# Branch outputs loaded and split ahead of the last gates' sigmoids, and both weightings of the dilated groups beside the first projection

## The chip, the cores and the metric

The kernel runs on one core of one Trainium2 chip, as one launch. The metric is the device time in microseconds (us) of one execution. Engines are called PE (TensorE), ACT (ScalarE), DVE (VectorE), POOL (GpSimd) and SP (SyncE); SP, POOL and ACT also issue DMAs from their queues.

## The reference, cut to what matters

One layer of an encoder, sequence 1024, width 1024, all in float32. From the normalized input `n` come three branches: A, dilated window attention in three head groups (dilation 1, 4, 16), whose group outputs are weighted by a softmax over their log-sum-exps; B, retention; C, cross-attention into 256 memory tokens. Each branch output is projected to 1024 columns, multiplied by a sigmoid gate and summed:

```python
alpha = jax.nn.softmax(jnp.stack(lses, axis=0), axis=0)
y = jnp.stack(outs, axis=0) * alpha[..., None].astype(q.dtype)
...
gates = jax.nn.sigmoid(n @ w_gate + b_gate).reshape(B, S, N_BRANCHES, D_MODEL)
merged = (gates[:, :, 0] * (y_a @ w_proj_attn)
          + gates[:, :, 1] * (y_r @ w_proj_ret)
          + gates[:, :, 2] * (y_m @ w_proj_mem))
h = h + merged @ w_out
```

A gated MLP with a short convolution and a final norm follow.

## The kernel before

All large products are made of three matmuls (`mm3`, L177 to L180): each float32 operand is split into a high and a low part, `hilo` (L182): ACT writes the high part (L183), DVE the rest (L184). Weights come by `WStream`: SP loads one of three `wraw` buffers (L222), `hilo` splits it into one of three `wh`/`wl` pairs, always for a column ahead. So each operand of PE passes SP, then ACT, then DVE.

The stage before the change is the gates: 12 pairs of gate columns, seven steps each (`gate_steps`, L1002 to L1065), 84 steps of 12 matmuls, merged evenly by `merge` with the 92 steps of the dilated attention (`attn_dil`). Of the last pair, the last step's sum is the function `late` (DVE at L1059, then two sigmoids on ACT at L1011, and stores to `sg_d` by POOL), called after the merged steps (L1176).

Then come the projections, one branch after the other, in `order`: b0 is retention (6 parts of 128 rows), b1 memory (4 parts), b2 the dilated attention (6 parts). `proj_steps` (L1187) has a step `begin`, in which `y_part` (L1069) loads each part of the branch output from DRAM into a `yraw` tile by SP and splits it into `yh` and `yl`, and eight steps `one(c)`, a column block each: 2 x 3 matmuls for each part into two PSUM banks (`accg`, six banks, so three columns), then DVE multiplies with the gate, loaded as `sg` by POOL (L1200), and adds to `mg`. The `yraw` tiles share the three buffers of the weights:

```python
r = W.rp.tile([P, S], F32, name="yraw", tag="wraw", bufs=3)
nc.sync.dma_start(r, y_src[bi][k * P:(k + 1) * P, :])
```

The 12 tiles of `yh`/`yl` are a pool `y_p`, opened after the gates. `sg`, the three U tiles of a weighting, and gate results are in the pool `ab` of eight buffers.

The weighting of the dilated groups is `combine(s)` (L885), for s = 0 and 1: `lse` (POOL loads three U tiles; ACT takes a logarithm, L896), `bcast(g)` for each group (DVE spreads the values into `lw`, L905, PE transposes them, L910, ACT copies them into L), and `comb(h)` for each half: maxima (L923, L924), differences (L926), exponentials on ACT (L927), products with U (L935), sums, two reciprocals (L931), products (L936), and stores into `ya_d` (L937), by POOL for s = 0 and by ACT's queue for s = 1. Its 12 steps are merged with the 18 steps of b0 and b1:

```python
run(merge(proj_steps(b0, k0) + proj_steps(b1, k1), combine(0, stats, cb_p) + combine(1, stats, cb_p)))
run(proj_steps(b2, k2))
```

A scheduler sets the final order of instructions on each engine; each engine then takes its queue in that order.

Of the kernel before, what the change touches and what calls it, by code (L numbers as in the profile page):

```python
# [11 lines left out]
F32 = mybir.dt.float32  # L12
# [5 lines left out]
P = 128  # L18
D = 1024
S = 1024  # L20
# [45 lines left out]
def merge(a, b):  # L66
    out, i, j = [], 0, 0
    while i < len(a) or j < len(b):
        if j >= len(b) or (i < len(a) and i * len(b) <= j * len(a)):
            out.append(a[i])  # L70
            i += 1
        else:
            out.append(b[j])
            j += 1
    return out


def run(steps):
    for s in steps:
        s()  # L80
# [65 lines left out]
def encoder_block(ctx: ExitStack, tc: tile.TileContext, x, mem, vec, w_mix, w_gate, w_pa, w_pr, w_pm,  # L146
                  w_out, w_mlp, g_final, t_rope, t_mask, t_ret, t_zeta, out):
    nc = tc.nc
# [3 lines left out]
    def pool(name, **kw):  # L152
        kw.setdefault("bufs", 1)
        return tc.tile_pool(name=name, reuse_waits="tile", **kw)
# [260 lines left out]
    pairs = PAIRS  # L415
# [469 lines left out]
    def combine(s, stats, ap_):  # L885
        loc = {}

        def lse():
            loc["st"] = [stats[3 * s + g] for g in range(3)]
            loc["U"] = [ab("U") for g in range(3)]  # L890
            for g in range(3):
                nc.gpsimd.dma_start(loc["U"][g], u_d[(3 * s + g) * P:(3 * s + g + 1) * P, :])
            loc["lse"] = ap_.tile([P, 3, 2, 8], F32, name="lse", tag="lse")
            for g in range(3):
                nc.vector.tensor_copy(loc["lse"][:, g], loc["st"][g][1])
            nc.scalar.activation(loc["lse"], loc["lse"], AF.Ln)  # L896
            for g in range(3):
                nc.vector.tensor_sub(loc["lse"][:, g], loc["lse"][:, g], loc["st"][g][0])
            loc["L"] = []

        def bcast(g):
            L = ap_.tile([P, S], F32, name="L", tag="L", bufs=3)
            for b in range(2):
                W2 = ap_.tile([P, 4, 2, 64], F32, name="lw", tag="sm", bufs=3)
                nc.vector.tensor_copy(W2, loc["lse"][:, g, :, 4 * b:4 * b + 4].rearrange("p h t -> p t h")  # L905
                                      [:, :, :, None].to_broadcast([P, 4, 2, 64]))
                ps = pst()
                for a in range(4):
                    t = 4 * b + a
                    nc.tensor.transpose(ps[:, a * P:(a + 1) * P],  # L910
                                        W2[:, a].rearrange("p a b -> p (a b)"), ident)
                if DIL[g] == 1:
                    nc.scalar.copy(L[:, b * HALF:(b + 1) * HALF], ps)
                else:
                    unperm(L, ps, DIL[g], b)
            loc["L"].append(L)

        def comb(h):
            c = slice(h * HALF, (h + 1) * HALF)
            L = [t[:, c] for t in loc["L"]]  # L920
            m = ap_.tile([P, HALF], F32, name="cm", tag="sm", bufs=3)
            z = ap_.tile([P, HALF], F32, name="cz", tag="sm", bufs=3)
            nc.vector.tensor_tensor(m, L[0], L[1], op=ALU.max)  # L923
            nc.vector.tensor_tensor(m, m, L[2], op=ALU.max)  # L924
            for g in range(3):
                nc.vector.tensor_sub(L[g], L[g], m)  # L926
                nc.scalar.activation(L[g], L[g], AF.Exp)  # L927
            nc.vector.tensor_add(z, L[0], L[1])
            nc.vector.tensor_add(z, z, L[2])
            for a in range(2):  # L930
                nc.vector.reciprocal(z[:, a * 256:(a + 1) * 256], z[:, a * 256:(a + 1) * 256])  # L931
            for g in range(3):
                u = loc["U"][g][:, c]
                k = 2 * g + s
                nc.vector.tensor_mul(u, u, L[g])  # L935
                nc.vector.tensor_mul(u, u, z)  # L936
                (nc.gpsimd, nc.scalar)[s].dma_start(ya_d[k * P:(k + 1) * P, c], u)  # L937

        return [lse] + [lambda g=g: bcast(g) for g in range(3)] + [lambda: comb(0), lambda: comb(1)]


    def attn_mem(h, qm, cp):
# [123 lines left out]

    y_src = {0: ya_d, 1: yr_d, 2: ym_d}

    def y_part(bi, k):  # L1069

        r = W.rp.tile([P, S], F32, name="yraw", tag="wraw", bufs=3)
        nc.sync.dma_start(r, y_src[bi][k * P:(k + 1) * P, :])
        a, b = (y_p.tile([P, S], F32R, name=t, tag="y", bufs=12) for t in ("yh", "yl"))
        hilo(a, b, r)
        return a, b
# [38 lines left out]
    T_s = ExitStack()  # L1114
# [56 lines left out]
    for k in range(KP):  # L1171
        hilo(*T1[k], t1[k])
    gates = sum((gate_steps(p, box, lambda: psW.tile([P, HALF], F32, name="w", tag="w", bufs=4))
                 for p in range(NG)), [])
    run(merge(gates, sum((attn_dil(i, ap_, stats) for i in range(len(pairs))), [])))
    box.pop("late")()  # L1176
    gs.close()
    T_s.close()


    pg = ExitStack()
    psG = pg.enter_context(pool("psG", space=PS))
    psb.update(pool=psG, bufs={"t": 2})
    cb_p = pg.enter_context(pool("cb_p", side="right"))
    y_p = pg.enter_context(pool("y_p"))
    mg = [n_p.tile([P, S], F32, name=f"mg{k}", tag="n", bufs=16) for k in range(KT - 1)] + [ab("mg")]
    mgh, mgl = [], []  # L1187

    def proj_steps(bi, kt):
        loc = {}  # L1190

        def begin():
            loc["y"] = zip(*[y_part(bi, k) for k in range(kt)])
            loc["y"] = list(loc["y"])

        def one(c):
            wh, wl = W.get()
            yh, yl = loc["y"]
            sg = ab("sg")
            nc.gpsimd.dma_start(sg, sg_d[(bi * KT + c) * P:(bi * KT + c + 1) * P, :])  # L1200
            ps = [psG.tile([P, HALF], F32, name="accg", tag="accg", bufs=6) for h in range(2)]
            for k in range(kt):
                for h in range(2):
                    cs = slice(h * HALF, (h + 1) * HALF)
                    mm3(ps[h], wh[:, k], wl[:, k], yh[k][:, cs], yl[k][:, cs], k == 0, k == kt - 1)
            if bi == order[2][0]:
                for r in (mgh, mgl):
                    r.append(n_p.tile([P, S], F32R, name=f"mg{c}", tag="n", bufs=16))
            for h in range(2):
                cs = slice(h * HALF, (h + 1) * HALF)  # L1210
                m = mg[c][:, cs]
                if bi == order[0][0]:
                    nc.vector.tensor_mul(m, ps[h], sg[:, cs])
                else:
                    nc.vector.tensor_mul(sg[:, cs], ps[h], sg[:, cs])
                    nc.vector.tensor_add(m, m, sg[:, cs])
                if bi == order[2][0]:
                    hilo(mgh[c][:, cs], mgl[c][:, cs], m)

        return [begin] + [lambda c=c: one(c) for c in range(KT)]  # L1220

    (b0, _, k0), (b1, _, k1), (b2, _, k2) = order
    run(merge(proj_steps(b0, k0) + proj_steps(b1, k1), combine(0, stats, cb_p) + combine(1, stats, cb_p)))
    run(proj_steps(b2, k2))
    pg.close()
    mk_s.close()

# [468 lines left out]
```

## Time and profile before

| | us |
|---|---|
| median of 3 runs | 1911.7 (1910.52 to 1913.72) |
| the profiled execution: time | 1913.29 |
| the profiled execution: span | 1911.5 |
| PE busy | 1849.1 (97%) |
| DVE busy | 1258.5 (66%) |
| ACT busy | 913.0 (48%) |
| POOL busy | 120.7 (6%) |

The span runs from the first to the last instruction of the one profiled execution. Busy time is the sum of an engine's instructions; a wait shows as idle time before an instruction, with the engine or DMA that ended it. `PEclk` is the granted clock of PE as a share of 2.4 GHz (0.50 is 1.2 GHz). In a timeline, consecutive instructions of one kind stand as one row with their count, and durations overlap by about 0.1 us, since an engine starts the next instruction before the last one's end.

### The profile page before, as it was taken

How to read it: one execution, taken by the hardware profiler on the slowest of the kernel's cores; microseconds unless marked ns; L12 is line 12 of the kernel's file. 1: busy time of each engine (PE TensorE's matmuls, PEld its weight loads, DVE VectorE, ACT ScalarE, POOL GpSimd, SP SyncE). 2: the span in 40 equal slices, each digit the busy share in tenths (PEclk: the TensorE clock that was granted, in tenths of full speed). 3: DMA queues.
4: the chain of work that ended last, by engine and by line, in shares of the span. 5: the costliest groups of instructions: out<-in, count | busy, mean ns of one | idle time of the engine just before them, and what ended most of it. 6: DMA issues, size and time to landing. Idle time of an engine off the chain costs nothing.

```text
span 1911.5 us, 24342 instructions
## 1 busy us (share of the span) xinstructions
PE 1849.1 (97%) x9314; PEld 1534.8 (80%) x9314; DVE 1258.5 (66%) x2192; ACT 913.0 (48%) x1498; POOL 120.7 (6%) x222
## 2 busy tenths in 40 slices
PE   7999999999999999999899699989999999999997
PEld 6889988888887777777687589967888888888886
DVE  7554463657455555555467864575888887899976
ACT  7354342435446556665533233552545454445444
POOL 1000010110000000000101000000000000020001
PEclk9999999999999999999999899989999999999999
DMA  6211111122331333223636525321223222287553
GB/s 245 94 54 45 45 54 47 67 78 89 110 110 67 111 127 115 100 78 110 214 123 214 200 87 186 119 82 54 90 77 100 79 87 89 77 341 264 171 165 116
DMA packets 65988, 223.69 MB, mean 117 GB/s; under 512 B 7760, under 2 KB 7888, under 8 KB 65744
## 3 DMA queue, kind: packets, MB, share of 16 engines
q1 hardware_dynamic: 41760, 138.77, 21.5%
q0 software_dynamic: 22096, 79.70, 11.0%
q10 hardware_dynamic: 2016, 3.67, 0.5%
q8 instruction: 73, 1.20, 0.3%
q14 instruction: 43, 0.35, 0.1%
HBM read 168.64 MB, written 53.48 MB: 116 GB/s over the span
## 4 chain that ended last, share of the span: by engine, by line
PE 91%; DVE 4%; DMA 2%; ACT 2%; issue 1%; POOL 0%; SPq 0%; POOLq 0%; ACTq 0%; DVEq 0%
PE ps L180 11%; PE ps L179 11%; PE ps L178 11%; PE acc L180 8%; PE acc L178 8%; PE acc L179 8%; PE w L178 5%; PE w L179 4%; PE w L180 4%; PE accg L178 2%; PE accg L179 2%; PE accg L180 2%; PE pss L810 2%; PE psu L854 2%; PE pso L179 2%; PE pso L180 2%
## 5 line engine op out<-in xcount | busy, mean ns | idle before, releaser
L183 ACT CAST wh<-wraw 128x1024 fp32r<-128x1024 f32 (+2 forms) x263 | 253.1, 967 | 326.6 <-PE acc L179 80.8
L184 DVE TENSOR_TENSOR wl<-wraw,wh 128x1024 fp32r<-128x1024 f32 (+2 forms) x263 | 293.8, 1118 | 150.0 <-ACT wh L183 145.2
L178 PE MATMUL acc<-nTh,wh 128*128 128x512 f32 x544 | 214.5, 394 | 0.0
L180 PE MATMUL acc<-nTh,wl 128*128 128x512 f32 x544 | 212.7, 391 | 0.0
L179 PE MATMUL acc<-nTl,wh 128*128 128x512 f32 x544 | 212.4, 390 | 0.0
L178 PE MATMUL ps<-wh,th 128*128 128x512 f32 x308 | 119.8, 389 | 0.0
L179 PE MATMUL ps<-wl,th 128*128 128x512 f32 x308 | 119.8, 389 | 0.0
L180 PE MATMUL ps<-wh,th 128*128 128x512 f32 x308 | 119.8, 389 | 0.0
L180 PEld LDWEIGHTS acc<-nTh,wl 128*128 128x128 f32 x544 | 102.2, 188 | 20.4
L178 PEld LDWEIGHTS acc<-nTh,wh 128*128 128x128 f32 x544 | 102.2, 188 | 20.2
L179 PEld LDWEIGHTS acc<-nTl,wh 128*128 128x128 f32 x544 | 102.3, 188 | 19.8
L179 PE MATMUL accg<-yl,wh 128*128 128x512 f32 x256 | 103.4, 405 | 11.2 <-DVE yl L184 11.0
L178 PE MATMUL accg<-yh,wh 128*128 128x512 f32 x256 | 98.8, 404 | 8.6 <-ACT yh L183 8.3
L539 ACT COPY sw<-acc 32x512 f32<-32x512 f32 x144 | 83.4, 579 | 49.1 <-PE acc L180 29.4
L180 PE MATMUL accg<-yh,wl 128*128 128x512 f32 x256 | 102.0, 400 | 0.5 <-DVE wl L184 0.5
L178 PE MATMUL w<-nTh,wh 128*128 128x512 f32 x192 | 79.2, 412 | 0.0
L179 PE MATMUL w<-nTl,wh 128*128 128x512 f32 x192 | 75.1, 391 | 0.0
L180 PE MATMUL w<-nTh,wl 128*128 128x512 f32 x192 | 75.0, 391 | 0.0
L178 PE MATMUL pso<-wh,mg 128*128 128x256 f32 x256 | 73.2, 286 | 0.0
L180 PE MATMUL pso<-wh,mg 128*128 128x256 f32 x256 | 72.5, 283 | 0.0
L179 PE MATMUL pso<-wl,mg 128*128 128x256 f32 x256 | 72.5, 283 | 0.0
L183 ACT CAST th<-g 128x512 fp32r<-128x512 f32 x66 | 40.9, 622 | 64.8 <-PE ps L180 45.4
(387 smaller groups left out, 4561.0 us busy)
## 6 DMA issues: line engine op xcount, KB each, us to landing
wraw<-in_w_mlp_dram SPq DMA_DIRECT2D x90, 512.0 KB, 4.0
wraw<-in_w_mix_dram SPq DMA_DIRECT2D x48, 512.0 KB, 3.5
wraw<-in_w_gate_dram SPq DMA_DIRECT2D x24, 512.0 KB, 3.5
sg<-sg_d POOLq DMA_DIRECT2D x24, 512.0 KB, 5.1
g_d<-cv POOLq DMA_DIRECT2D x22, 512.0 KB, 2.9
g<-g_d POOLq DMA_DIRECT2D x22, 512.0 KB, 14.3
wraw<-in_w_out_dram SPq DMA_DIRECT2D x16, 512.0 KB, 4.0
sg_d<-ub POOLq DMA_DIRECT2D x12, 512.0 KB, 2.9
```

The lines of the kernel that those rows point to most:

```text
L178: nc.tensor.matmul(o, lh, rh, start=first, stop=False, **kw)
L179: nc.tensor.matmul(o, lh, rl, start=False, stop=False, **kw)
L180: nc.tensor.matmul(o, ll, rh, start=False, stop=last, **kw)
L183: nc.scalar.copy(hi, src)
L184: nc.vector.tensor_sub(lo, src, hi.bitcast(F32))
L539: nc.scalar.copy(sw[q * 32:(q + 1) * 32], ps[o * 32:(o + 1) * 32])
L810: nc.tensor.matmul(ps[:, a * w:(a + 1) * w], st["q"][r, q0:q0 + P], st["k"][r, k0:k0 + w], start=True, stop=True)
L854: nc.tensor.matmul(u[64 * i:64 * i + 64, c], loc["V"][:, vslot[k0 + k * P], 64 * i:64 * i + 64], pt[:, k, a], start=k == 0, stop=k == nk - 1)
```

## The change

`combine`'s step `bcast` is cut in two, `spread` (DVE's part) and `bcast` (PE and ACT), so that a weighting has nine steps. The `yraw` tiles move from the weights' buffers to the pool `ab`. The last four gate steps are run after the merged list, which now merges 80 gate steps with the 92 of the attention; three parts of b0 are loaded ahead of those four steps, the pool `y_p` opens after them (in the space of `T_p`, the gates' operands), the rest of b0 is loaded and all of it split, and only then `late` is called. Both weightings, 18 steps, are merged with the nine steps of b0. Two parts of b1 are loaded before b1's steps, four of b2 before its last two.

```diff
-        def bcast(g):
-            L = ap_.tile([P, S], F32, name="L", tag="L", bufs=3)
+        def spread(g):
+            loc["w"] = []
             for b in range(2):
                 W2 = ap_.tile([P, 4, 2, 64], F32, name="lw", tag="sm", bufs=3)
                 nc.vector.tensor_copy(W2, loc["lse"][:, g, :, 4 * b:4 * b + 4].rearrange("p h t -> p t h")
                                       [:, :, :, None].to_broadcast([P, 4, 2, 64]))
+                loc["w"].append(W2)
+
+        def bcast(g):
+            L = ap_.tile([P, S], F32, name="L", tag="L", bufs=3)
+            for b, W2 in enumerate(loc.pop("w")):
                 ps = pst()
...
-        return [lse] + [lambda g=g: bcast(g) for g in range(3)] + [lambda: comb(0), lambda: comb(1)]
+        steps = [lambda g=g, f=f: f(g) for g in range(3) for f in (spread, bcast)]
+        return [lse] + steps + [lambda: comb(0), lambda: comb(1)]
...
-    def y_part(bi, k):
-
-        r = W.rp.tile([P, S], F32, name="yraw", tag="wraw", bufs=3)
+    def y_raw(bi, k):
+        r = ab("yraw")
         nc.sync.dma_start(r, y_src[bi][k * P:(k + 1) * P, :])
+        return r
+
+    def y_part(r):
+
         a, b = (y_p.tile([P, S], F32R, name=t, tag="y", bufs=12) for t in ("yh", "yl"))
         hilo(a, b, r)
         return a, b
...
-    run(merge(gates, sum((attn_dil(i, ap_, stats) for i in range(len(pairs))), [])))
+    b0, b1, b2 = (b for b, _, _ in order)
+    y_r = {}
+
+    def y_load(bi, ks):
+        for k in ks:
+            y_r[bi, k] = y_raw(bi, k)
+
+    run(merge(gates[:-4], sum((attn_dil(i, ap_, stats) for i in range(len(pairs))), [])))
+    y_load(b0, range(3))
+    run(gates[-4:])
+    T_s.close()
+    pg = ExitStack()
+    y_p = pg.enter_context(pool("y_p"))
+    y_hl = {}
+
+    def y_split(bi, kt):
+        y_load(bi, [k for k in range(kt) if (bi, k) not in y_r])
+        y_hl[bi] = list(zip(*[y_part(y_r.pop((bi, k))) for k in range(kt)]))
+
+    y_split(b0, order[0][2])
     box.pop("late")()
     gs.close()
-    T_s.close()
...
         def begin():
-            loc["y"] = zip(*[y_part(bi, k) for k in range(kt)])
-            loc["y"] = list(loc["y"])
+            if bi not in y_hl:
+                y_split(bi, kt)
...
-    (b0, _, k0), (b1, _, k1), (b2, _, k2) = order
-    run(merge(proj_steps(b0, k0) + proj_steps(b1, k1), combine(0, stats, cb_p) + combine(1, stats, cb_p)))
-    run(proj_steps(b2, k2))
+    s0, s1, s2 = (proj_steps(bi, kt) for bi, _, kt in order)
+    run(merge(s0, combine(0, stats, cb_p) + combine(1, stats, cb_p)))
+    y_load(b1, range(2))
+    run(s1[:-2])
+    y_load(b2, range(4))
+    run(s1[-2:] + s2)
```

What a scheduler makes of it is seen in the built order of each engine. Where a row ends in a count, that many follow each other; line numbers behind the change are those of the changed file.

**ACT at the end of the gates, before.** `ub` and `ua` are the last gate pair, `lse` belongs to the first weighting, `wh` are weights of b0.

```order
L1046 COPY ub<-w 128x512
L839 COPY pt_s<-pst 128x256
L183 CAST wh<-wraw 128x768
L883 COPY U<-psu 128x8x64
L1011 ACT_TABLE_LOAD
L1011 ACTIVATE ub<-ub,vec 128x1024
L1011 ACTIVATE ua<-ua,vec 128x1024
L896 ACT_TABLE_LOAD
L896 ACTIVATE lse<-lse 128x48
L183 CAST yh<-yraw 128x1024
L183 CAST wh<-wraw 128x768
```

The same place with the change:

```order
L896 ACT_TABLE_LOAD
L896 ACTIVATE lse<-lse 128x48
L1047 COPY ua<-w 128x512
L1051 COPY ub<-w 128x512
L183 CAST wh<-wraw 128x768
L183 CAST yh<-yraw 128x1024
L1016 ACT_TABLE_LOAD
L1016 ACTIVATE ub<-ub,vec 128x1024
L183 CAST yh<-yraw 128x1024
L1016 ACTIVATE ua<-ua,vec 128x1024
L183 CAST yh<-yraw 128x1024
L183 CAST wh<-wraw 128x768
```

The logarithm has moved ahead of the last copies; one cast of a part of b0 stands ahead of the first sigmoid, one between the two, the other four behind.

**DVE at the split of b1's parts, before** (`yl` are the low halves of the parts, `U`, `cz`, `L`, `cm` the weighting, `mg` and `sg` the products of a column). The end of the first weighting stands here:

```order
L931 RECIPROCAL cz<-cz 128x256 x2
L935 TENSOR_TENSOR U<-U,L 128x512
L1213 TENSOR_TENSOR mg_7825<-accg,sg 128x512 x2
L936 TENSOR_TENSOR U<-U,cz 128x512 x3
L184 TENSOR_TENSOR wl<-wraw,wh 128x512
L184 TENSOR_TENSOR yl<-yraw,yh 128x1024
L184 TENSOR_TENSOR wl<-wraw,wh 128x512
L905 COPY lw<-lse 128x512 x3
L1213 TENSOR_TENSOR mg<-accg,sg 128x512
L184 TENSOR_TENSOR yl<-yraw,yh 128x1024
L1213 TENSOR_TENSOR mg<-accg,sg 128x512
L184 TENSOR_TENSOR yl<-yraw,yh 128x1024 x2
```

The same place with the change, from the first half's last products of the second weighting on:

```order
L940 TENSOR_TENSOR U<-U,cz 128x512 x3
L928 TENSOR_TENSOR cm<-cm,L 128x512
L184 TENSOR_TENSOR yl<-yraw,yh 128x1024
L930 TENSOR_TENSOR L<-L,cm 128x512 x3
...
L935 RECIPROCAL cz<-cz 128x256 x2
L184 TENSOR_TENSOR yl<-yraw,yh 128x1024
L940 TENSOR_TENSOR U<-U,cz 128x512 x3
L184 TENSOR_TENSOR yl<-yraw,yh 128x1024
L184 TENSOR_TENSOR wl<-wraw,wh 128x512
L184 TENSOR_TENSOR yl<-yraw,yh 128x1024
```

Here the second weighting stands, whose second half has come between b1's first and second part, with its last products between the second and third. The first half stands ahead of all of them.

## Rows read from the trace of the kernel before

**Rows 1.** The page's first line, the span of the profiled execution.

```profile
span 1911.5 us, 24342 instructions
```

**Rows 2.** Busy times by stage: gates' end, b0, b1, b2; then PEclk, DMA share, GB/s.

```profile
core 0: us, PE busy (x) PEld busy (x) DVE busy (x) ACT busy (x) POOL busy (x), PEclk, DMA share, GB/s
860.00:936.20 76.20, 76.20 (x378) 58.58 (x376) 39.25 (x107) 46.22 (x86) 6.39 (x12) 1.00 0.39 140
936.20:1017.30 81.10, 73.31 (x318) 59.74 (x318) 51.90 (x82) 26.79 (x33) 10.21 (x19) 0.96 0.45 151
1017.30:1069.30 52.00, 49.16 (x211) 38.64 (x210) 40.07 (x60) 15.44 (x20) 4.38 (x9) 0.93 0.62 223
1069.30:1152.40 83.10, 69.23 (x289) 54.52 (x290) 54.10 (x75) 23.54 (x32) 2.64 (x5) 0.94 0.38 136
```

**Rows 3.** What PE waited for from 936 to 1153: total us, times, longest.

```profile
PE accg L179 <- DVE yl L184: 11.0, 3, 10.0
PE accg L178 <- ACT yh L183: 8.3, 7, 3.4
PE pst L910 <- DVE lw L905: 4.2, 1, 4.2
```

**Rows 4.** The projections' matmuls alone in a steady stretch of b2.

```profile
1100.00:1150.00 50.00, 50.00 (x222) 41.42 (x221) 8.14 (x12) 1.00 0.27 90
```

**Rows 5.** Timeline of PE: start, us, instruction, count [idle before].

```profile
973.27 1.03 PE L910 MATMUL pst<-ident,lw 128*128 128x128 f32 x8
...
1081.64 0.80 PE L179 MATMUL accg<-yl,wh 128*128 128x512 f32 x1 [9.99 <-DVE yl L184]
1082.24 0.63 PE L180 MATMUL accg<-yh,wl 128*128 128x512 f32 x1
1082.66 0.63 PE L179 MATMUL accg<-yl,wh 128*128 128x512 f32 x1
```

**Rows 6.** Timeline of DVE, end of b0's split and the weighting before b2.

```profile
961.89 1.23 DVE L184 TENSOR_TENSOR yl<-yraw,yh 128x1024 fp32r<-128x1024 f32 x1 [1.87 <-ACT yh L183]
...
1069.33 1.89 DVE L926 TENSOR_TENSOR L<-L,cm 128x512 f32<-128x512 f32 x3
...
1077.97 1.89 DVE L936 TENSOR_TENSOR U<-U,cz 128x512 f32<-128x512 f32 x3
...
1080.37 1.22 DVE L184 TENSOR_TENSOR yl<-yraw,yh 128x1024 fp32r<-128x1024 f32 x1
```

**Rows 7.** Timeline of SP's queue, the loads of b2's parts.

```profile
1064.38 26.23 SPq L1072 DMA_DIRECT2D yraw<-ya_d  x6
```

**Rows 8.** Timeline of ACT, end of the gates, and one strided copy pair.

```profile
932.44 0.83 ACT L183 CAST wh<-wraw 128x768 fp32r<-128x768 f32 x1 [2.66 <-PE w L179]
...
934.34 1.28 ACT L1011 ACT_TABLE_LOAD   x1
935.63 1.15 ACT L1011 ACTIVATE ub<-ub,vec 128x1024 f32<-128x1024 f32 x1
...
938.12 1.28 ACT L896 ACT_TABLE_LOAD   x1
939.41 0.24 ACT L896 ACTIVATE lse<-lse 128x48 f32<-128x48 f32 x1
939.79 1.05 ACT L183 CAST yh<-yraw 128x1024 fp32r<-128x1024 f32 x1
...
1039.91 2.04 ACT L883 COPY L<-pst 128x512 f32<-128x512 f32 x2
```

**Rows 9.** The page's DMA issues: KB each, median us from issue to landing.

```profile
sg<-sg_d POOLq DMA_DIRECT2D x24, 512.0 KB, 5.1
```

**Rows 10.** Short stretches; the column before DMA share is PEclk.

```profile
940.00:944.00 4.00, 3.44 (x10) 2.49 (x11) 3.38 (x7) 2.15 (x3) 1.07 (x2) 0.65 0.76 267
...
1082.00:1084.00 2.00, 2.00 (x6) 1.52 (x6) 1.06 (x2) 0.00 (x0) 1.52 (x3) 0.50 0.90 285
1088.00:1092.00 4.00, 3.02 (x12) 1.68 (x11) 1.62 (x2) 2.05 (x2) 0.00 (x0) 1.00 1.03 415
```

More of the change, by code (lines that the diff above doesn't have):

```diff
@@ L906, in bcast @@
                                       [:, :, :, None].to_broadcast([P, 4, 2, 64]))
+                loc["w"].append(W2)
+        def bcast(g):
+            L = ap_.tile([P, S], F32, name="L", tag="L", bufs=3)
+            for b, W2 in enumerate(loc.pop("w")):
                 ps = pst()
                 for a in range(4):
-                    t = 4 * b + a
                     nc.tensor.transpose(ps[:, a * P:(a + 1) * P],
@@ L1174, in encoder_block @@
                  for p in range(NG)), [])
-    run(merge(gates, sum((attn_dil(i, ap_, stats) for i in range(len(pairs))), [])))
+    b0, b1, b2 = (b for b, _, _ in order)
[14 more added lines that the diff above has]
+    y_split(b0, order[0][2])
     box.pop("late")()
     gs.close()
-    T_s.close()
-    pg = ExitStack()
     psG = pg.enter_context(pool("psG", space=PS))
@@ L1184, in encoder_block @@
     cb_p = pg.enter_context(pool("cb_p", side="right"))
-    y_p = pg.enter_context(pool("y_p"))
     mg = [n_p.tile([P, S], F32, name=f"mg{k}", tag="n", bufs=16) for k in range(KT - 1)] + [ab("mg")]
@@ L1189, in proj_steps @@
     def proj_steps(bi, kt):
-        loc = {}
         def begin():
-            loc["y"] = zip(*[y_part(bi, k) for k in range(kt)])
-            loc["y"] = list(loc["y"])
+            if bi not in y_hl:
+                y_split(bi, kt)
         def one(c):
             wh, wl = W.get()
-            yh, yl = loc["y"]
+            yh, yl = y_hl[bi]
             sg = ab("sg")
```

## The prediction

> **What bounds the kernel now.** The page gives the span of the profiled execution, 1911.5 us [rows 1]; its own time is 1913.29 us, so 1.8 us lie around the span. Busy time by stage comes next, cut at each stage's last matmul [rows 2]: TensorE (PE) works without a gap while the gates are computed (76.2 of 76.2 us, clock 1.00), and it is short of work in each of the three projections: 73.3 of 81.1 us in the first (b0, retention), 49.2 of 52.0 in the second (b1, memory), 69.2 of 83.1 in the third (b2, dilated). What PE waits for there is nearly always a half of a branch output: `yl` from VectorE (DVE) 11.0 us, `yh` from ScalarE (ACT) 8.3 us, and the broadcast weights `lw` 4.2 us [rows 3]. So these stages are bound by how early the branch outputs are split, and everything else in the kernel runs as the change leaves it.
>
> **What the three starts cost.** A steady matmul of a projection takes 50 us / 222 = 0.226 us (the 222 count both cut ends) [rows 4], eight transposes of the weighting 0.8 us [rows 5]. So b0 needs 288 x 0.226 = 65.1 us plus 24 transposes (2.4) = 67.5 and takes 81.1, a loss of 13.6. b1 needs 192 x 0.226 + 2.4 = 45.8 and takes 52.0: loss 6.2. b2 needs 65.1 and takes 83.1: loss 18.0. That is 37.8 us together, the most that could be won. The largest is b2's: its first `yl`, a split that takes 1.2 us, stands in DVE's queue behind a whole half of `comb` and starts at 1080.37 [rows 6], while PE stands for 9.99 us [rows 5]; the six loads are spread over 26.2 us on SP's queue, because they share three buffers with the weights and wait for the weighting to be written [rows 7].
>
> **First start (b0).** Loads are no longer in the way: three are queued before the last four gate steps, three directly after. But the order built for ACT (shown with the change) has, after the weight cast that waits for the sixth gate step, only one `yh` before the sigmoid's table load; the sigmoids and the next casts alternate. The four last gate steps now run alone, 12 matmuls or 2.7 us each, and I let them end at 936.2 as before, so that weight cast starts at 933.4. From there on ACT's queue, by durations in [rows 8]: cast of a weight 0.83, `yh` 1.05, table 1.28, sigmoid 1.15, `yh` 1.05, sigmoid 1.15, `yh` 1.05, weight 0.83, `yh` 1.05, two copies of L 1.1 (an estimate at half the two-copy row, which is of the strided kind), `yh` 1.05, `yh` 1.05: 12.6 us, less about 0.1 of overlap at each of ten = 11.7, so 945.1; the last `yl` (1.2, a little late because DVE also forms `lw` between) at 947. Before, it ended at 961.89 + 1.23 = 963.1 [rows 6]. By 947 PE has had 31 of the first 72 matmuls to do and has waited some 3 us. The other 41 take 9.3 us, eight transposes 0.8, the third column 8.1: done at 965.2, against 973.27 before [rows 5]. **8.1 us won here.** The Trainium skill (ScalarE: Activation LUTs, What ACT_TABLE_LOAD costs) puts a drain of 1.38 us on top of the 1.28 us load, which would make this chain 1.4 us longer; the trace has the next ACTIVATE 1.29 us after the load's start [rows 8], so nothing is added.
>
> **Rest of b0.** Five columns are left: 40.7 us. All 48 transposes of both weightings now lie in b0, so 32 are still to come instead of 16: 3.2 us (1.6 more, taken from b1). DVE is the new doubt: beside b0's own splits and products it gets both weightings. One half of `comb` is 11.1 us: from 1069.33 to 1077.97 + 1.89 is 10.5 [rows 6], less one product (0.6) that stands among it, plus its two maxima (1.2). Four halves are 44 us. The products have three columns of PSUM to fall behind, so PE doesn't stop for them; in the built order the second weighting's `lw` come behind the second half of the first `comb`, and there I count 1.2 us of waiting in column c=6. POOL's queue gets the second weighting's three loads of U, and the first one's stores, among the `sg` loads: three stores stand ahead of the `sg` of c=5, three ahead of that of c=6. The first half of that `comb` is done about 979 (965.2, transposes and copies 2.9, then 11.1), the second with what stands between about 992; an `sg` load lands 5.1 us after its issue [rows 9], before its column ends at 992 and 1001. So that queue costs nothing; if it did, a product would be late, and PE has three columns of room. So c=6 ends at 965.2 + 4 x 8.15 + 2.4 + 1.2 = 1001.4 and b0 at 1010.4, against 1017.2.
>
> **Second start (b1), where most of that goes again.** The built order puts b1's four `yl` among the two halves of the second `comb`: one behind the first half, the second behind the second half's reciprocals, two behind its end. That `comb` can't start before the transposes that stand between c=6 and c=7 are copied out: 1001.4 + 0.9 + two strided copies 2.0 [rows 8] = 1004.3. Then DVE has without a break: two halves 22.2 (less one maximum done ahead, 0.6), two products 1.2, four splits at 1.14 = 4.6, one weight split 0.6: 28.0 us, to 1032.3. ACT has its own hold: three stores of `ya_d` wait in its queue for the first half's products, ahead of the second `yh`, and three more ahead of the fourth; both end before DVE gets there. PE does the 36 matmuls that earlier parts allow and starts the other 156 about 1.2 us late, because after such waits it runs at 1.2 GHz (clock 0.50, matmuls 0.43 us apart) [rows 5, 10]: 1033.5 + 156 x 0.226 = 1068.8, against 1069.3. **So at the end of b1 almost nothing is left of the lead (0.5 us).** The weighting that stopped b2 now stops b1.
>
> **Third start (b2).** `ya_d` is complete at about 1032, its loads are queued during b1. Two of six parts have free tiles and are split early; the others need tiles that b1's last column releases one after another, which the built order follows: four parts are split when b2 starts, the fifth about 3.6 us and the sixth 4.8 us after (that column's sums 2.4, a split 1.2 each), while PE needs them after 24 and 30 matmuls, 5.4 and 6.8 us. No wait: 65.1 instead of 83.1. **18.0 us won.** The loads and the six buffers moved to the other pool cost nothing while b1's 35 us cover them; without that cover b2 would wait for a load again, at most the 18 us.
>
> **Sum.** 0.5 + 18.0 = 18.5; I take 18, since the strided copies and the clock are rounded in favour. 1913.3 - 18 = 1895.3 for an execution like the profiled one, which was 1.6 above the median of the runs shown: **1894 us**.
>
> **Rivals.**
> - *DVE keeps up* and b1 starts with its parts split, as the change means it: b0's lead of 6.8 us stays, b1 takes 43.4 + 2 instead of 52.0, b2 65.1: 31 us won, 1881. Against it stands DVE's order. Chance 0.10.
> - *Slow clock in both broken stretches.* The 31 matmuls and 8 transposes before 947 would take 31 x 0.427 + 1.6 = 14.8 us, 4 more than there is room for, and the resumption in b1 2 more: 1898 to 1900. For it: clock 0.65 at 940 to 944 after a long wait. Against it: at 1088 to 1092, PE with gaps under 1 us and 3.0 of 4 us busy, the clock is 1.00 [rows 10]. The Trainium skill (TensorE: Matmul & The Clock Gate, HAM oscillation) describes work in bursts with waits between as starting each burst at the lower clock; by that rule the change would get this price. Chance 0.13.
> - *b2's wait stays in part*: the loads of its last parts hang on `sg` buffers that b1's columns release and stand in SP's queue behind weights. A third to all of the 18 us comes back: 1900 to 1912. Chance 0.12, half of it within 0.2% of no change.
> - *Slower.* The gates' stage, idle-free so far, gets 92 attention steps into 80 gate steps instead of 84, and other positions of every step. If the chain scores, exponentials, transposes then misses its turn in each of the 12 gate pairs, PE stops there. It decides from 18 / 12 = 1.5 us a pair; at 2 us it would be 1894 + 24 = 1918. For it: ACT holds each pair's two sigmoids with table loads of 1.28 [rows 8]; against it: no idle PE time at all in that stage, DVE and ACT about half idle [rows 2]. Chance 0.05.
> - *The change doesn't do what it says* for the early split: five of six `yh` still follow a sigmoid. If the last parts then came as late as before, b0's start would win nothing, and DVE's chain and b1's end would shift by up to 7 us: 1901. Chance 0.05, inside the range.
>
> **How the numbers follow.** The forecast's own chance is 0.55, 1889 to 1899 (PE's resumption and DVE's chain each some 3 us uncertain). With the clock rival, the late-split rival and *DVE keeps up* (whose middle is the lower end) the range is 1881 to 1902. A measurement here can tell 0.2%, 3.8 us, from no change. Faster by more: 0.55 + 0.10 + 0.13 + 0.05 + about 0.06 = 0.89; within: 0.06; slower: 0.05.
>
> **What would show it.** In the new profile: `yl` of b0 done near 947 and PE's idle time there under 5 us; PE again waiting for `yl` near 1012 to 1032, with reciprocals and U products on DVE in that stretch; clock 0.5 there; b1's end near 1069; no wait over 1 us at b2's start, and its last matmul near 1134 instead of 1152. It would be wrong if b1's matmuls run dense from about 1015, if `yl` of `ya_d` is waited for again, or if the gates' stage shows idle PE.

## The result and the profile after

The changed kernel takes **1890.8 us** (median of 4 runs, 1890.1 to 1895.4) against 1911.7 (1910.5 to 1913.7): ratio 0.9895, 95% interval 0.9882 to 0.9907. Run once more beside other kernels it took 1893.5 us (1890.1 to 1896.4), ratio 0.9895 (0.9873 to 0.9917). The profiled execution took 1895.35 us, 17.9 less than that of before (1913.29) and the longest of its four. One execution of e11 below took 4963 us, far from its other three (1901.1 to 1901.9), and is not counted.

The page's first lines, span and busy times (engine, us, share, count):

```profile
span 1893.4 us, 24355 instructions
...
PE 1843.2 (97%) x9314; PEld 1532.5 (81%) x9314; DVE 1256.5 (66%) x2192; ACT 906.2 (48%) x1494; POOL 120.4 (6%) x222
```

Busy time by stage, cut at the last matmul of each (gates' end, b0, b1, b2), and two short stretches, to be laid beside [rows 2]; columns as there:

```profile
core 0: us, PE busy (x) PEld busy (x) DVE busy (x) ACT busy (x) POOL busy (x), PEclk, DMA share, GB/s
857.40:933.60 76.20, 76.20 (x372) 59.46 (x370) 39.63 (x112) 46.95 (x84) 3.72 (x7) 1.00 0.42 152
933.60:1007.10 73.50, 71.96 (x337) 58.51 (x335) 55.93 (x85) 31.45 (x41) 11.95 (x22) 1.00 0.57 197
1007.10:1067.10 60.00, 49.17 (x194) 39.17 (x195) 49.04 (x68) 16.57 (x21) 6.08 (x12) 0.91 0.63 217
1067.10:1132.00 64.90, 64.90 (x288) 53.72 (x287) 38.49 (x57) 16.16 (x23) 2.35 (x5) 1.00 0.33 111
934.00:944.00 10.00, 9.37 (x42) 7.08 (x43) 8.14 (x10) 8.46 (x10) 3.62 (x7) 1.00 0.89 295
1015.00:1031.00 16.00, 11.13 (x30) 7.99 (x31) 13.51 (x17) 3.81 (x5) 2.06 (x4) 0.71 0.44 140
```

PE waits little in b0 and not at all in b2 now; b1 is longer than before. What PE waits for from 933 to 1133 (total us, times, longest), beside [rows 3]:

```profile
PE accg L179 <- DVE yl L184: 10.1, 5, 4.6
PE accg L178 <- ACT yh L183: 1.4, 1, 1.4
PE pst L914 <- DVE lw L905: 0.7, 1, 0.7
```

Of the 10.1 us, 9.4 stand in b1, and so does the wait for `yh`. DVE's timeline shows why (start, us, instruction, count): its queue runs from the second weighting's maximum to b1's last `yl` without a gap.

```profile
1000.49 0.69 DVE L928 TENSOR_TENSOR cm<-cm,L 128x512 f32<-128x512 f32 x1 [1.16 <-ACT L L883]
...
1013.45 1.22 DVE L184 TENSOR_TENSOR yl<-yraw,yh 128x1024 fp32r<-128x1024 f32 x1
...
1019.40 3.36 DVE L935 RECIPROCAL cz<-cz 128x256 f32<-128x256 f32 x2
1022.67 1.16 DVE L184 TENSOR_TENSOR yl<-yraw,yh 128x1024 fp32r<-128x1024 f32 x1
...
1027.29 1.22 DVE L184 TENSOR_TENSOR yl<-yraw,yh 128x1024 fp32r<-128x1024 f32 x1
```

The table gives each branch's length in the profiled execution of every kernel, counted by matmuls (288, 192 and 288; a boundary between branches is good to about 1 us, and in two rows b0's end is read from the first wait of b1), the sum from the gates' end to the first matmul behind b2, and the median time. The gates' stage itself is told of at the end.

| kernel | b0 | b1 | b2 | sum | time |
|---|---|---|---|---|---|
| before | 79.8 | 53.2 | 83.1 | 216.1 | 1911.7 |
| changed | 73.5 | 60.0 | 64.9 | 198.4 | 1890.8 |
| e1 weighting back, 18 steps | 69.8 | 58.0 | 94.5 | 222.3 | 1919.5 |
| e2 late split of b0 | 73.1 | 59.8 | 64.5 | 197.4 | 1891.9 |
| e3 b1 split first | 73.5 | 52.6 | 65.1 | 191.2 | 1888.3 |
| e4 stores by POOL | 73.5 | 58.6 | 65.3 | 197.4 | 1898.4 |
| e5 changed, again | 73.5 | 60.0 | 65.1 | 198.6 | 1893.5 |
| e6 all but the pool | 78.0 | 58.8 | 66.2 | 203.0 | 1901.7 |
| e7 the pool alone | 69.5 | 49.4 | 74.1 | 193.0 | 1891.1 |
| e8 weighting cut finely | 73.5 | 52.7 | 69.6 | 195.8 | 1890.0 |
| e9 weighting back, 12 steps | 69.9 | 49.4 | 76.4 | 195.6 | 1891.4 |
| e10 pool for b0 alone | 69.6 | 54.1 | 82.8 | 206.5 | 1901.4 |
| e11 pool for b1 and b2 | 79.8 | 49.4 | 74.6 | 203.7 | 1901.2 |
| e12 weighting by mid b1 | 69.9 | 60.6 | 65.1 | 195.7 | 1891.0 |

Two things are needed to read it. The cut at 1017.3 in [rows 2] stands behind six matmuls of b1 (318 there are 288, 24 transposes and 6), so that the kernel before has 79.8 and 53.2 by count where that row has 81.1 and 52.0. And b0 holds all 48 transposes of the weightings in the changed kernel and in e2 to e6 (40 in e8), 24 in the others: 2.4 us more in b0 and less in b1, at 0.8 us for eight.

In all fourteen profiled executions the span less the gates' stage and this sum lies between 1340.3 and 1344.9 us: what these executions differ in by more than 5 us lies in these stages. A median moves by 2 or 3 us for reasons outside them, so effects under 4 us are read from the stages.

### The profile page after: what moved, and what is told of

Read it like the earlier page. It is cut to its first block, busy times and chain, and to the rows that moved or that the text cites. A ratio compares the mean times of both kernels' runs of the same rounds, so it can differ in the third digit from the quotient of the medians.

```text
span 1893.4 us, 24355 instructions
## 1 busy us (share of the span) xinstructions
PE 1843.2 (97%) x9314; PEld 1532.5 (81%) x9314; DVE 1256.5 (66%) x2192; ACT 906.2 (48%) x1494; POOL 120.4 (6%) x222
## 4 chain that ended last, share of the span: by engine, by line
PE 91%; DVE 5%; ACT 2%; issue 1%; DMA 0%; POOL 0%; SPq 0%; POOLq 0%; ACTq 0%; DVEq 0%
PE ps L180 11%; PE ps L179 11%; PE ps L178 11%; PE acc L180 8%; PE acc L178 8%; PE acc L179 8%; PE w L178 5%; PE w L179 4%; PE w L180 4%; PE accg L179 2%; PE accg L180 2%; PE accg L178 2%; PE psu L854 2%; PE pss L810 2%; PE pso L180 2%; PE pso L179 2%
## 5 line engine op out<-in xcount | busy, mean ns | idle before, releaser
L179 PE MATMUL accg<-yl,wh 128*128 128x512 f32 x256 | 101.9, 399 | 10.1 <-DVE yl L184 10.1
```

What stands on the lines that cost most here:

```text
L179: nc.tensor.matmul(o, lh, rl, start=False, stop=False, **kw)
```

## The experiments

The first four ask what each named move of the change is worth.

**e1: the weighting merged with b0 and b1 again.**

```diff
-    run(merge(s0, combine(0, stats, cb_p) + combine(1, stats, cb_p)))
-    y_load(b1, range(2))
-    run(s1[:-2])
-    y_load(b2, range(4))
-    run(s1[-2:] + s2)
+    run(merge(s0 + s1, combine(0, stats, cb_p) + combine(1, stats, cb_p)))
+    run(s2)
```

> One part undone: the two weightings are merged again with the 18 steps of b0 and b1 and b2 gets its loads without hints, while the early loads and splits of b0 and the other pool for yraw stay. Theory (DVE's queue: where a half of the weighting stands, the next branch starts late): b0 keeps its gain, about 74 us; a half of the first weighting stands at b1's split, so b1 takes about 52; the last half of the second stands again ahead of b2's yl, PE waits about 10 us there and b2 takes 80 to 84. Time 1903 us (1900 to 1906), 12 above the changed kernel's median of 1890.8. Rival (b2's gain came from taking the loads out of the weights' buffers): b2 stays near 66 us and the time near 1891.

Measured: 1919.5 us (1918.7 to 1920.3), ratio to before 1.004 (1.0025 to 1.0055): slower than before. b2 took 94.5 us; 21.7 us of the waits below (what PE waits for in e1, 934 to 1160) stand there, and they hang on DVE's queue and on loads issued behind its last stores:

```profile
PE accg L178 <- ACT yh L183: 12.8, 2, 7.4
PE accg L179 <- DVE yl L184: 7.4, 6, 2.8
PE accg L180 <- DVE wl L184: 5.7, 1, 5.7
PE accg L178 <- DVE sg L1237: 4.4, 1, 4.4
```

This was no undo of one part: cut into 18 steps instead of 12, the merged weighting ends 21 us behind b1's last matmul, where it ended 11 behind in the kernel before. e9 repeats it cleanly.

**e2: b0 split late.** The gates merged whole, the late sum first, `begin` loads and splits b0.

```diff
-    run(merge(gates[:-4], sum((attn_dil(i, ap_, stats) for i in range(len(pairs))), [])))
-    y_load(b0, range(3))
-    run(gates[-4:])
+    run(merge(gates, sum((attn_dil(i, ap_, stats) for i in range(len(pairs))), [])))
+    box.pop("late")()
...
-    y_split(b0, order[0][2])
-    box.pop("late")()
```

> The other part undone: all 84 gate steps are merged with the attention as before, the late sum and its sigmoids come first, and b0's parts are loaded and split only then; both weightings stay beside b0. Theory (b0's start is worth its own 7 to 8 us, and everything after it, DVE's chain into b1 too, hangs on PE's place in b0 and moves with it): b0 takes about 81 us, b1 59, b2 66; time 1898 us (1896 to 1900). Rival (DVE's chain of both weightings has a pace of its own, so that b1's end does not move and b0's lead is lost in b1 in any case): 1891 to 1893, with b1 at 52. Second rival (the last four gate steps alone also save something in the gates): 1 to 2 us more, gates ending that much later than at 933.6.

Measured: 1891.9 us (1891.2 to 1894.0). The theory fell: b0 keeps its 73 us although the program loads and splits it later. SP's timeline shows that its loads still go out ahead of the gates' end (934.8), since their buffers are free:

```profile
919.40 0.42 SPq L1076 DMA_DIRECT2D yraw<-yr_d  x1
...
922.65 3.31 SPq L1076 DMA_DIRECT2D yraw<-yr_d  x5
```

Before, SP issued the six over 22.9 us from 934.9 on. Among what it waited for there (the kernel before, 925 to 962: us in total, times, longest) are the splits that read a weight (`wl`) or an earlier part (`yl`) and so give one of the three shared buffers back:

```profile
SPq L1072 <- DVE wl L184: 10.3, 1, 10.3
SPq L1072 <- DVE yl L184: 7.9, 4, 2.4
```

In e2 no load of b0 has such a wait. Of the rivals, the first has the time but not b1's length (59.8 us, not 52); the second held: the gates' stage is 352.6 us again instead of 351.5. The medians, 1.1 us apart, can't tell.

**e3: b1's split ahead of the last half.**

```diff
-    run(merge(s0, combine(0, stats, cb_p) + combine(1, stats, cb_p)))
-    y_load(b1, range(2))
-    run(s1[:-2])
+    cmb = combine(0, stats, cb_p) + combine(1, stats, cb_p)
+    run(merge(s0, cmb[:-1]))
+    y_split(b1, order[1][2])
+    run(s1[:1] + cmb[-1:] + s1[1:-2])
```

> One thing moved: b1's parts are loaded and split ahead of the last half of the second weighting, whose place is then among b1's first column. Theory (b1 waits for DVE, where one half of the weighting stands among its splits): the last yl of b1 comes about 9 us earlier, near 1019 instead of 1028.5 on the trace's clock; PE waits under 3 us for yl in b1 instead of 9.4; b1 takes 50 to 52 us instead of 59; b2 still without a wait since ya_d is stored by about 1030; time 1883 us (1881 to 1886). Rival (b1's matmuls are slow by the clock and not by DVE): 1888 to 1890, with matmuls 0.43 us apart after 1015 as now. Rival (the weighting moved behind the split stops b2 again): PE waits for yl of ya_d at b2's start, time 1887 to 1891.

Measured: 1888.3 us (1885.0 to 1889.3), ratio 0.9874 (0.9857 to 0.9890). On DVE the four splits stand among the differences of the last half:

```profile
1012.77 1.22 DVE L184 TENSOR_TENSOR yl<-yraw,yh 128x1024 fp32r<-128x1024 f32 x1
...
1015.71 2.36 DVE L184 TENSOR_TENSOR yl<-yraw,yh 128x1024 fp32r<-128x1024 f32 x2
...
1018.58 1.22 DVE L184 TENSOR_TENSOR yl<-yraw,yh 128x1024 fp32r<-128x1024 f32 x1
```

The last `yl` ends at 1019.8 instead of 1028.5, b1 takes 52.6 us instead of 60.0, and b2 does not wait. So DVE's order set b1's start. PE still waits 4.2 us for the first `yl`, more than I expected, and the time stays above the 1881 to 1886 expected: the stages won 7.2 us, the medians only 2.5 (against 1890.8) to 5.2 (against e5).

**e4: the second weighting's stores by POOL's queue.**

```diff
-                (nc.gpsimd, nc.scalar)[s].dma_start(ya_d[k * P:(k + 1) * P, c], u)
+                nc.gpsimd.dma_start(ya_d[k * P:(k + 1) * P, c], u)
```

> One queue changed: the second weighting's stores of ya_d go out by POOL's queue like the first's, so that ACT's casts of b1's parts no longer stand behind them. Theory (DVE has its 28 us without a break and sets the last yl): the yh come up to 8 us earlier and wait for DVE; yl, b1 and the time stay, 1890.8 us (1889 to 1892). Rival (ACT's queue, held by the stores, sets b1's start): PE's waits for yl in b1 fall from 9.4 to 4 or 5 us, time 1885 to 1887. Rival (the sg loads of b1 then stand behind six stores on POOL's queue): products late by more than three columns, time above 1893.

In the projections the theory holds: PE's two long waits for `yl` in b1 are 4.57 and 3.74 us (4.56 and 4.32 in the changed kernel), the sum is 197.4. But the time is 1898.4 us (1895.5 to 1899.9), as in the last rival, whose late products the projections do not show. The profile, of the shortest of the four executions, has 1.95 us of it behind the projections, a wait for `hs` at 1181.5 that no other profile has; the rest stays open.

With the changed kernel's second run as their base, e6 and e7 take the pool apart, since e2 pointed there, and e8 tries another place for the weighting.

**e5: the changed kernel again.**

> The changed kernel once more, as the base of the runs beside it: its profiled execution took 4.6 us more than its other three. Theory (that is scatter of single executions, at the start and behind the projections, and not in them): median 1890 to 1893; gates end to the last projection matmul again 198.4 us within 0.5. Rival (the long execution shows a wait of the change that comes and goes in the projections): that stretch differs from 198.4 by over 2 us.

Measured: 1893.5 us, just above the 1890 to 1893 expected, and 198.6 us from the gates' end to b2's end. The scatter lies outside.

**e6: all of the change but the pool.**

```diff
-        r = ab("yraw")
+        r = W.rp.tile([P, S], F32, name="yraw", tag="wraw", bufs=3)
```

> One part undone: the yraw tiles share the three buffers of the weights again, all else as in the changed kernel. Theory, from the run with the late split (which kept b0's gain of 7 us though it loaded and split b0 after the sigmoids): the gain at b0's start is that of the buffers, since six loads then needn't wait in turn for three buffers. So b0 takes 79 to 82 us again with yl some 2.6 us apart, and b2's six loads take turns as well and PE waits there 5 to 10 us in pieces; time 1903 us (1897 to 1910). Rival (my prediction: the early place in the program gives b0's start its gain, and the buffers cost or give nothing while they are covered): 1891, b0 at 73 to 75.

Measured: 1901.7 us (1900.1 to 1904.8), ratio 0.9945 (0.9928 to 0.9962). b0 loses 4.5 us again with `yl` 2.3 to 6.7 us apart, b1's first wait grows to 6.7 us; b2 waits 0.5 us only, against what I expected: with the weighting done early, three buffers are enough there. SP issues b0's first load at 933.7, though the program has it ahead of the last four gate steps; the longest wait before these loads (8.3 us) is again for `wl`. What PE waits for, then b0's last `yl` on DVE:

```profile
PE accg L179 <- DVE yl L184: 10.9, 3, 6.7
PE accg L178 <- ACT yh L183: 3.6, 2, 2.5
...
960.93 1.16 DVE L184 TENSOR_TENSOR yl<-yraw,yh 128x1024 fp32r<-128x1024 f32 x1
```

**e7: the pool alone.** The same line, changed in the kernel before and nothing else:

```diff
-        r = W.rp.tile([P, S], F32, name="yraw", tag="wraw", bufs=3)
+        r = ab("yraw")
```

> One part alone: the kernel before with nothing changed but the yraw tiles taken from the pool of eight buffers. Theory (the buffers give b0's start its 7 us, and the weighting's place gives b2's 17): b0 takes 73 to 75 us; b1's parts come early and it takes 47 to 52; but the second half of the second weighting ends near b1's end and the six loads of b2 follow it, so that PE waits 10 to 18 us at b2's start; time 1904 us (1898 to 1910). Rival (the buffers give b2 its gain too, since its loads can run ahead): below 1897, no wait over 3 us in b2. Rival (the buffers give nothing without the early place): 1910 to 1913, b0 at 81.

Measured: **1891.1 us** (1888.6 to 1892.3), ratio 0.9886 (0.9870 to 0.9902). One line gives as much as the whole change. The theory's 1904 fell; the first rival's time came, with one wait of 4.0 us left in b2, but its reason, b2's loads running ahead, did not. What PE waits for in its projections, then b0's last `yl` on DVE:

```profile
PE accg L178 <- DVE sg L1215: 4.0, 1, 4.0
PE accg L179 <- DVE yl L184: 1.7, 1, 1.7
...
943.89 2.35 DVE L184 TENSOR_TENSOR yl<-yraw,yh 128x1024 fp32r<-128x1024 f32 x2
```

SP issues all six of b0's loads by 925.4 and b1's four in 2.4 us (18.1 before). With b1's loads ready, the built order of DVE puts all of the second weighting's `lw` ahead of b1's first `yl`, where they stood among b1's splits and products, so that its last half ends 3 us behind b1's last matmul instead of 11:

```profile
1004.88 1.19 DVE L905 COPY lw<-lse 128x512 f32<-128x512 f32 x3
...
1008.41 1.23 DVE L184 TENSOR_TENSOR yl<-yraw,yh 128x1024 fp32r<-128x1024 f32 x1 [0.17 <-ACT yh L183]
...
1050.65 3.35 DVE L931 RECIPROCAL cz<-cz 128x256 f32<-128x256 f32 x2
...
1059.53 1.22 DVE L184 TENSOR_TENSOR yl<-yraw,yh 128x1024 fp32r<-128x1024 f32 x1
```

The last row is b2's first `yl`, which stands at 1080.37 in the kernel before [rows 6].

**e8: the second weighting cut into six pieces beside b1.** Both `comb` halves are returned as three functions each (`fine`), left out of the merge with b0. The lines that this replaces, and slices that are empty, are left out here:

```diff
+    run(merge(s0, w0 + w1[:-2]))
+    y_split(b1, order[1][2])
+    run(s1[:1] + merge(s1[1:7], fine))
+    y_load(b2, range(4))
+    run(s1[7:] + s2)
```

> A version meant to beat both: the two comb halves of the second weighting are cut in three pieces each (differences, sums, products with stores), b1's parts are loaded and split ahead of all six, and these are merged with b1's first six columns. Theory (DVE's queue sets b1's start and its work has room beside b1's columns): the last yl of b1 near 1012 instead of 1028.5, PE's waits in b1 under 4 us instead of 10.8, b1 47 to 49 us instead of 59; ya_d stored by about 1046, b2 waits up to 3 us; time 1880 us (1878 to 1885). Rival (the weighting ends too late for b2's loads, now that b1 is shorter): PE waits 5 us or more at b2's start, time 1885 to 1890. Rival (DVE is over-full in b1, since products of six columns and 20 us of weighting don't fit into 34 us): PE waits for PSUM banks late in b1, time above 1886.

Measured: 1890.0 us (1889.7 to 1893.3). b1 gained 7 us, b2 lost 5: mainly the first rival, at the upper end of its time, though PE's waits in b2 come to 3.6 us and not 5, with a touch of the second, since PE waits 2.0 us for `wl` at b1's end. DVE is busy without a break from 1030 to 1055 and the weighting ends too late for b2's loads.

The last four undo the weighting's move cleanly, separate what the pool does for b0 from what it does later, and try one more place for the weighting.

**e9: the weighting as before, 12 uncut steps** (the lines that the last two replace are those of e1).

```diff
-        steps = [lambda g=g, f=f: f(g) for g in range(3) for f in (spread, bcast)]
+        steps = [lambda g=g: (spread(g), bcast(g)) for g in range(3)]
...
+    run(merge(s0 + s1, combine(0, stats, cb_p) + combine(1, stats, cb_p)))
+    run(s2)
```

> The weighting's move undone cleanly, with its 12 uncut steps merged with b0 and b1 as before, while the other pool, the early loads and the early split of b0 stay (the first undo, with 18 cut steps, put the last half one to two columns later than before). Theory, from the run with the pool alone (projections 193.0 us, 5 less than the changed kernel's 198.4): gates' stage 351.5 us like the changed kernel's, b0 71, b1 48, b2 70 to 73; projections 192 to 194, time 1889 us (1887 to 1892). Rival (my prediction: b2's gain needs the weighting beside b0): PE waits 10 us for the first yl of b2 and the time is near 1903.

Measured: 1891.4 us (1890.4 to 1892.0). The weighting's move is worth nothing beside the pool: against e5 it costs b0 3.6 (24 transposes among it) and b1 10.6 us and gives b2 11.3.

**e10 and e11: the pool for b0 alone, and for the others alone.** In the kernel before; e11 has `!=` in place of `==`:

```diff
-        r = W.rp.tile([P, S], F32, name="yraw", tag="wraw", bufs=3)
+        r = ab("yraw") if bi == order[0][0] else W.rp.tile([P, S], F32, name="yraw", tag="wraw", bufs=3)
```

> The kernel before with only b0's six yraw tiles in the pool of eight; b1's and b2's stay in the weights' three buffers. Theory (the buffers act twice: in b0 on the loads, and through b1's loads on the place of the second weighting, whose transposes the built order here has again behind b1's splits): b0 72 us instead of 81, b1 46 to 52, b2 again 80 to 84 with 8 to 10 us of waiting for its first yl; time 1904 us (1902 to 1907). Rival (b0's earlier end alone pulls the second weighting ahead of b2): 1891 to 1896.

> The complement: b0's tiles stay in the weights' three buffers, those of b1 and b2 go to the pool of eight. Theory: b0 80 to 82 us as before, b1 about 48, b2 70 to 73, since the second weighting's second half ends beside b1's last columns; time 1898 us (1896 to 1901), and this gain and that of the run with b0's tiles alone add up to the 20.5 us of the pool alone. Rival (b2 gains because its own six loads are issued together): the weighting stands where it did, DVE's wait before b2's first yl stays, and b2's gain is under 8 us: 1904 or more.

Measured: 1901.4 us (1899.4 to 1904.1), ratio 0.9951 (0.9935 to 0.9966), and 1901.2 us (1901.1 to 1901.9), 0.9948 (0.9929 to 0.9968), both just outside what was expected. e10 has b0 at 69.6 us and the old wait ahead of b2, e11 the reverse. What PE waits for, first e10, then e11:

```profile
PE accg L179 <- DVE yl L184: 11.6, 4, 10.1
PE accg L178 <- ACT yh L183: 5.7, 6, 1.3
```

```profile
PE pst L910 <- DVE lw L905: 4.2, 1, 4.2
PE accg L178 <- ACT yh L183: 4.1, 3, 3.7
PE accg L178 <- DVE sg L1215: 4.0, 1, 4.0
```

The two gains nearly add up: 9.6 + 12.4 = 22.0 us in the stages, where the pool alone has 23.1.

**e12: the weighting by the middle of b1.** As e9, with other limits of the merge (the new lines):

```diff
+    run(merge(s0 + s1[:5], combine(0, stats, cb_p) + combine(1, stats, cb_p)))
+    run(s1[5:7])
+    y_load(b2, range(4))
+    run(s1[7:] + s2)
```

> A version meant to beat both: as the clean undo, but the weighting's 12 steps are merged with b0 and only b1's first four columns, and four of b2's loads stand ahead of b1's last two columns. Theory (DVE is short of room only where a whole half stands before a split or the products; spread over b0 and half of b1 it has room, and ya_d is stored some 12 us before b2): gates' stage 351.5, b0 71 to 72, b1 48 to 50, b2 66 to 67 without a wait; projections 186 to 189, time 1882 to 1886. Rival (DVE over-full in b1, as in the finely cut version, where it was busy without a break from 1020 to 1055): products or weight splits late, PE waits 4 us or more late in b1; time 1889 to 1893.

Measured: 1891.0 us (1890.0 to 1893.9): the rival. In the middle of b1 DVE has not a moment free and PE works 12.9 of 20 us:

```profile
1030.00:1050.00 20.00, 12.86 (x51) 10.02 (x52) 20.00 (x31) 3.87 (x6) 0.00 (x0) 0.92 0.42 144
```

## Why the prediction was right, and where it was not

**The size.** 1894 was forecast, 1890.8 came, inside the range. Execution against execution it is 1913.3 - 17.9 where the sum had 18; the runs of the changed kernel scatter by 5 us, and the profiled one lies at their upper end. That the whole meets the sum to 0.1 us is in part luck: the three projections gave 17.7 where their terms add up to 18.5, and 1.1 came from the gates' stage, which is in no term.

**The gates' end** was taken as 936.2 and came at 933.6. 1.5 us of that is an earlier start of the stage, which varies between executions (580.5 to 583.8); 1.1 is the stage itself.

**First start.** ACT's chain came in the order and length worked out. From the weight cast to the end of the last `yl` it took 13.4 us, against 13.6 in the sum (ACT's timeline, then DVE's):

```profile
930.74 0.84 ACT L183 CAST wh<-wraw 128x768 fp32r<-128x768 f32 x1 [1.95 <-PE w L179]
931.48 1.05 ACT L183 CAST yh<-yraw 128x1024 fp32r<-128x1024 f32 x1
932.55 1.28 ACT L1016 ACT_TABLE_LOAD   x1
933.84 1.15 ACT L1016 ACTIVATE ub<-ub,vec 128x1024 f32<-128x1024 f32 x1
...
940.46 2.00 ACT L183 CAST yh<-yraw 128x1024 fp32r<-128x1024 f32 x2
```

```profile
941.77 2.35 DVE L184 TENSOR_TENSOR yl<-yraw,yh 128x1024 fp32r<-128x1024 f32 x2
```

The next ACTIVATE stands 1.29 us after the table load's start, and the cast ahead of the load ends where it starts. The drain that the Trainium skill (ScalarE: Activation LUTs, What ACT_TABLE_LOAD costs) adds does not show here either. **The step that failed** is the cause of this gain: I put 8.1 us down to the early place in the program, "three are queued before the last four gate steps", and priced the pool at nothing. b0's last `yl` ends 27.1 us after the gates' end before and 10.7 in the changed kernel. In e6, with the early place and without the pool, it ends at 28.1; in e2, e7 and e10, with the pool and without the early place, at 12.3. In b0's length e6 loses 4.5 us; what it keeps of the gain is not the splits': 16 transposes of the weightings run in it while PE has no part of b0. e7 and e10, which hold 2.4 us of transposes less, have more than the changed kernel's gain (69.5 and 69.6 against 73.5).

The loss at b0's start was also a little too large: by count b0 lost 12.3 us and b1 7.4, not 13.6 and 6.2, because the cut took six matmuls of b1 for b0's. The three together stay 37.7.

**Rest of b0.** 73.5 us against 74.2; the wait for `lw` in c=6 was 0.7 us, not 1.2.

**Second start.** DVE's unbroken chain lasted from 1000.49 to 1028.5, 28.0 us as summed, and b1 took 60.0 us against 58.4. e3 shows that the chain was the cause, e4 that ACT's stores were not. After the first long wait PE's matmuls start 0.43 us apart for some 2 us, then 0.23; after the second, of 4.32 us, the lower clock lasts longer (PE's timeline, then a stretch with the columns of [rows 2]):

```profile
1014.72 0.79 PE L179 MATMUL accg<-yl,wh 128*128 128x512 f32 x1 [4.56 <-DVE yl L184]
1015.31 0.63 PE L180 MATMUL accg<-yh,wl 128*128 128x512 f32 x1
1015.74 0.63 PE L179 MATMUL accg<-yl,wh 128*128 128x512 f32 x1
...
1024.50:1031.00 6.50, 5.95 (x15) 4.16 (x14) 4.01 (x5) 1.04 (x1) 1.43 (x3) 0.51 0.84 264
```

So the clock was the term that the sum had too small here: when the last `yl` ended, PE had done 30 of the 36 matmuls that the sum let it do, and the rest of b1 took some 38 us where the sum had 36.5. That is the clock rival's part for b1, "the resumption in b1 2 more". Its larger part fell: in b0's start, with waits of under 1 us, the granted clock stayed at 1.00 (the stretch 934 to 944 above). The Trainium skill's case (TensorE: Matmul & The Clock Gate, HAM oscillation) has waits longer than the bursts of work between them; the prediction stretched it to b0's short waits, and only b1's waits of 4.6 and 4.3 us bear it out.

**Third start.** No wait, 64.9 us against 65.1. The reading of the changed kernel was right, but not that b2's 18 us need the weighting's move. By e7 and e9 the pool alone wins most of what the three starts lose, and the move then trades b1's time for b2's and costs 3.0 us in the sum (198.6 against 195.6). By e6 the moves do win when the pool is missing: 216.1 to 203.0. These are two remedies for the same waits: the moves alone take 13.1 us out of the stages, the pool alone 23.1, and both together 17.7.

Of the rivals, *DVE keeps up* is nearest to what e7 does in b1 (49.4 us), where little of the second weighting stands ahead of b1's last split, and in the changed kernel both its halves. *The change doesn't do what it says* was half true: the early split adds nothing, but its price didn't come, since the pool brought the parts in time. Beside the clock in b1, no other came. The shortest of all kernels is e3, whose slowest run (1889.3) is under the fastest of the changed kernel's eight (1890.1); from e7 it is 1.8 us apart in the stages, and their ratios (0.9874 and 0.9886) lie within each other's intervals.

## What to carry to other kernels

When a change gives loads buffers of their own and also moves code, price and run the buffers alone first: here one line carried 20.5 us, and the two moves that name the change added nothing to it. No run tells whether it matters that the buffers are those of another pool, or only that there are more of them. Once the buffers were free, SP issued b0's loads some 12 us before the gates' end though the program places them behind it (e2 and e7); the early place brought three of them forward to 893 and did not shorten b0 further (73.5 us against 73.1). And where DVE worked 20.0 of 20 us (e12), moving its work had only shifted the wait from one stage to another; what helped was a better order of what is urgent within it (e3).

## What was not expected

The last four gate steps, run alone instead of merged with the attention, shorten the gates' stage: 351.5 us in the nine profiled executions built that way, 352.6 in the five others, with the same work. PE's waits there are 0.3 us in the first group and none in the second, so it is no wait that went. The traces place it in the score matmuls (`pss`, L810) that follow each other: their starts lie 0.197 us apart on average in the changed kernel (146 pairs) and 0.210 before (144), 1.5 us in all. Why was not tested.

The pool's effect on b2 came mainly through the built order and not through b2's own loads: those are still issued behind the weighting, in e7 five of six from 1057.8 on, and the same five from 1085.4 on in e1, where b2 takes 94.5 us with the same pool. No run gives the pool to b1 or to b2 alone, so what b2's own buffers add is not separated: these five loads start within 1.9 us in e7 and within 9.5 in the kernel before.
